# Windowed attention scored by half blocks of 320 keys, with start-up splits and tail loads in another order

## The chip, the cores and the metric

The kernel runs on one core of one Trainium2 chip. The metric is the device time of one execution in microseconds (us). Three executions of the kernel before took 2492.85, 2494.92 and 2496.40 us; the median, 2494.92 us, is the time that the forecast is made against.

## The reference, cut to what matters

One encoder layer is applied to two sequences (prompt and sample) of 2048 tokens by 1024 channels, all in float32.

- `h = rms_norm(x)`, then one projection of 1024 by 3328 gives q, k, v and a gate for two groups of heads.
- Group A (stage one of the kernel): 8 query heads and 2 key/value heads of 64 channels. A query sees the keys at most 128 tokens before or behind it. q and k are normalised and partly rotated; a learned sink per head joins the maximum and the denominator of the softmax.
- Group B (stage two): 8 heads, neighbourhood attention on a grid of 32 by 64 tokens with a learned bias.
- Each group's output is multiplied by SiLU of its gate; both together go through `w_out` and are added to x; then `x + (p @ w_ple) * sigmoid(x @ w_ple_gate)` (stage three).

The change is in group A:

```python
sc = einsum('bqkgd,bskd->bkgqs', qb, kb) * scale     # 128 queries, 384 keys
sc = where(abs(s - 128 - q) <= 128 and key exists, sc, -inf)
m = maximum(max(sc), sink);  e = exp(sc - m)
o = (e / (sum(e) + exp(sink - m))) @ vb
```

Of the 384 keys that a block of 128 queries is scored with, each query sees 257; 64 neighbouring queries see 320 between them.

## The kernel before, in words

Every float32 product is made of two or three products of a rounded part and a rest: an operand is split by ScalarE (ACT) into `hi`, and VectorE (DVE) or GpSimd (POOL) makes `lo = x - hi`. TensorE (PE) then multiplies hi by hi, hi by lo, and mostly lo by hi, into one PSUM tile.

**Stage one** (`f` from 0 to 31; 16 blocks of 128 tokens for each sequence, `s, t = divmod(f, 16)`). `proj_a(f)` is a generator that makes the projection of block f: 24 products of 256 columns for k and v (`pk`), 24 of 512 for q (`pq`), 24 of 512 for the gate (`pg`). It is the filler between the steps of attention, `unit_a(f, kv)`, one unit for each of the two key heads of a block. A unit has these steps: `sc(i)` (scores of one query head against 384 keys, two products, then on DVE mask and row maximum in `softmax`, L275), `exps` (L291 on ACT, denominator on DVE, gate factor g2 on POOL), `pt(j)` (four transposes of 128 by 128 for one block of keys, a copy on ACT and the rest on DVE into a `p_t` tile, L678 and L679), `po(j)` (two products of 512 columns with the values), `fin` (transposed gate, sums of two halves of rows on ACT and DVE, L698 to L702, store).

`PLAN_A` is an order written out by hand: a list of (share of the filler's cost, this or the previous unit, step, index). The main loop draws filler products until the share is reached and then emits the step, so that TensorE always has projection products between two steps. The order of TensorE's instructions is pinned to that emission. On the other engines the framework's scheduler may place an instruction earlier or later, unless `P` (keep in program order) or `behind` (not before the present product) fixes it. SyncE (SP) issues nearly all DMAs, in one queue.

PSUM has three groups of banks: `pj` (3 banks: projections), `sc` (3 banks, shared by `sc`, `pt` and `pgt`) and `ms` (2). With eight uses of `sc` in a unit, a score's bank is the one used three steps before: the third score's bank held the last `pt` of the unit before, the fourth's held the first score.

At an edge of a sequence (t = 0 or 15) two key blocks are there instead of three: 256 keys.

**Start.** SP loads x, the weights of `pk` (`wx`), of `pq` (`w_q`), the rows for the norms (`n`), the rotation tables (`cs`, `rw`), the weights of `pg` (`w_g`). `split_w` (L156 on ACT, L157 on DVE) splits each weight block. Block 0 and 1 make their `pk`, then their `pq`, then their `pg`.

**Stage two** (`f` from 32 to 95) works the same way with `proj_b` and `unit_b`; each unit loads its values (`vw`, L825) from DRAM. At the end of each stage two blocks are projected together (`paired`), so that the weights' tiles come free early.

**Tail.** While the last units of stage two run, `ple_ahead(n)` makes `p @ w_ple`, tile by tile of 512 tokens (8 groups `m` of 6 products), copies it from PSUM to an `ev` tile (L953) and stores it (`ple_d`, L954). Between these, `load_coming` loads the split blocks of `w_out` named a11, a12, a22 (L930), 512 KB each, one at every odd m.

Of the kernel before, what the change touches and what calls it, by code (L numbers as in the profile page):

```python
# [11 lines left out]
F32 = mybir.dt.float32  # L12
# [88 lines left out]
def emit(ctx, tc, io):  # L101
# [24 lines left out]
    nc.vector.tensor_tensor(out=wk[:, 0:1], in0=wkt[:, 0:1], in1=wkt[:, 1:2], op=ALU.mult)  # L126
    nc.vector.tensor_tensor(out=wk[:, 1:2], in0=wkt[:, 2:3], in1=wkt[:, 3:4], op=ALU.mult)
    nc.vector.tensor_scalar_mul(wk, wk, 0.125)
    nc.vector.memset(wk[0:16, 0:1], 0.125)
    nc.vector.memset(wk[64:80, 0:1], 0.125)  # L130
# [122 lines left out]
    def behind(ins):  # L253

        tc.add_manual_dep(ins.ins, last_pe[-1].name,
                          mybir.DependencyInfo(mybir.DependencyClass.NoSync, mybir.DependencyReason.DATA),
                          reason="behind the product")
# [14 lines left out]
    def softmax(i, ps, n, bias, sm):  # L272

        s = main.tile([128, 512], F32, tag="s", name="s", bufs=SB)
        nc.vector.tensor_tensor_reduce(out=s[:, :n], in0=ps[:, :n], in1=bias, scale=1.0, scalar=-3.0e38,  # L275
                                       op0=ALU.add, op1=ALU.max, accum_out=sm["mx"][:, i:i + 1])
        sm["s"].append(s)
# [4 lines left out]
    def exps(sm, n, fct, gs, sink=None):  # L282

        mx, nm, den, rd, ss = (sm[k] for k in ("mx", "nm", "den", "rd", "s"))
        if sink is None:
            nc.vector.tensor_scalar_mul(nm, mx, -1.0)  # L286
            yield
        else:
            nc.vector.scalar_tensor_tensor(out=nm, in0=mx, scalar=-1.0, in1=sink[1], op0=ALU.mult, op1=ALU.min)
        for n_, i in enumerate((0, 2, 1, 3) if sink is None else range(4)):  # L290
            ex = nc.scalar.activation(ss[i][:, :n], ss[i][:, :n], AF.Exp, bias=nm[:, i:i + 1],  # L291
                                      accum_out=den[:, i:i + 1])
            if sink is None and n_ == 0:
                P(ex)
        if sink is not None:
            es = ap.tile([128, 4], F32, tag="es", name="es", bufs=3)
            nc.vector.tensor_tensor(out=es, in0=sink[0], in1=nm, op=ALU.add)
            nc.scalar.activation(es, es, AF.Exp)
            yield
            nc.vector.tensor_tensor(out=den, in0=den, in1=es, op=ALU.add)  # L300
# [99 lines left out]
    raws_q += load_first(raw[:, 0:2], 2, 256, 512)  # L400
    for i in range(2):
        load_block(("n", 0, i), "s", SB)
    raws_q += load_first(raw[:, 2:4], 4, 256, 512)
# [14 lines left out]
    raws_q += load_first(main.tile([128, 2, 512], F32, tag="p_t", name="ws", bufs=3), 6, 256, 512)  # L418
    for j in range(KT // 2):
        split_w(w_q[j], raws_q[j], nw[:, j:j + 1])  # L420
    for i in range(2):
        square(0, i)
    for i in range(2):
        square(1, i)
# [15 lines left out]
    nc.sync.dma_start(snk[:, 0, :], io["sink"].partition_broadcast(128))  # L440
    nc.vector.tensor_scalar_mul(snk[:, 1, :], snk[:, 0, :], -1.0)
    tab = [ap.tile([128, 2, NT, 16], F32, tag="vp", name=f"tab{i}", bufs=3) for i in range(2)]
# [7 lines left out]
    mask = ap.tile([128, 384], F32, tag="vp", name="mask", bufs=3)  # L450
# [32 lines left out]
    def proj_a(f):  # L483
# [5 lines left out]
        for i, c in enumerate(project(pk, xr, lambda k, b: wx[:, k, b, :], 112)):  # L489
            if i in HS and early:  # L490
# [6 lines left out]
        nc.scalar.activation(sq2[:, :128], pk[:, 0:128], AF.Square)  # L497
        nc.vector.tensor_reduce(out=ssq[:, 8:10], in_=sq2[:, :128].rearrange("p (h d) -> p h d", d=HD),
                                op=ALU.add, axis=AX.X)
# [34 lines left out]
        for i, c in enumerate(project(pq, xr, lambda k, b: w_q[k][:, b, :], 215)):  # L534
# [6 lines left out]
            if i == PV:  # L541
                values()
# [98 lines left out]
    def prep_a(f):  # L641
        q = held[f][0]
        pqt = ptile([128, 512], "ms", "pqt")
        for i in range(4):
            tr(pqt[:, 128 * i:128 * i + 128], q[:, 2 * i:2 * i + 2, :].rearrange("p h d -> p (h d)"))
# [4 lines left out]
        return q1, q2  # L650

    def unit_a(f, kv):
        s, t = divmod(f, NT)
        _, gs, y = held[f]
        k0, k1 = max(0, t - 1), min(NT, t + 2)
        n = 128 * (k1 - k0)
        m0 = 128 * (k0 - t + 1)
        sm, prs, got = sm_tiles(), [], {}

        def sc(i):  # L660
            ps = ptile([128, 512], "sc", "sc")
            for j, q in enumerate(qs[f]):
                mm(ps[:, :n], q[kv][:, 128 * i:128 * i + 128], ks_a[:, kv, 128 * k0:128 * k1], j == 0, j == 1)
            softmax(i, ps, n, mask[:, m0:m0 + n], sm)
            if i == 3:
                got["ex"] = exps(sm, n, y[:, 11:12], gs[:, 256 * kv:256 * kv + 256],
# [3 lines left out]
        def pt(j):  # L670
            if j >= k1 - k0:
                return
            pt = ptile([128, 4, 128], "pt", "pt")
            for i in range(4):
                tr(pt[:, i, :], sm["s"][i][:, 128 * j:128 * j + 128])
            pr = main.tile([128, 2, 512], F32R, tag="p_t", name="pr", bufs=3)
            pf = pt.rearrange("p h q -> p (h q)")
            nc.scalar.copy(pr[:, 0], pf)  # L678
            nc.vector.tensor_tensor(out=pr[:, 1], in0=pf, in1=pr[:, 0].bitcast(F32), op=ALU.subtract)  # L679
            prs.append(pr)  # L680

        def po(j):
            if j == 0:
                got["po"] = ptile([128, 512], "ms", "po")
            if j < k1 - k0:
                v = vv[:, k0 + j, kv].rearrange("p a d -> p (a d)")
                for i in range(2):
                    mm(got["po"], v, prs[j][:, i], j == 0 and i == 0, k0 + j == k1 - 1 and i == 1)

        def fin(_):  # L690
# [4 lines left out]
            ph2 = got["po"].rearrange("p (i e q) -> p e i q", e=2, q=128)  # L695
            for e in range(2):
                a, z = 64 * e, 64 - 64 * e
                nc.scalar.copy(ot[a:a + 64], ph2[z:z + 64, e])  # L698
            for e in range(2):
                a = 64 * e  # L700
                nc.vector.tensor_tensor(out=ot[a:a + 64], in0=ph2[a:a + 64, e], in1=ot[a:a + 64], op=ALU.add)
# [106 lines left out]
    def unit_b(f):  # L808
# [25 lines left out]
        def sc(h):  # L834
# [5 lines left out]
            if h == 3:  # L840
                got["ex"] = exps(sm, n, hr_b[:, st:st + 1], gs)
# [92 lines left out]
    def ple_ahead(n, tail=False):  # L934

        load_p(n + 1)
        for m in range(KT):
            if m % 2:
# [12 lines left out]
            else:  # L951
                ev = ap.tile([128, TW], F32, tag=("ev", "sq")[m // 2 % 2], name="ev", bufs=2)
# [27 lines left out]
    for count, w, raws in ((24, (), ()), (24, w_q, raws_q), (10 ** 9, w_g, raws_g)):  # L980
        if w is w_q:
            for j in range(KT // 2, KT):
                split_w(w[j], raws[j], nw[:, j:j + 1])
# [12 lines left out]
    def paired(f, n):  # L996
# [7 lines left out]
        else:  # L1004
            load_early("p")
            load_coming(4)
# [9 lines left out]
        else:  # L1016
            for name in ("a11", "a12", "a22"):
# [256 lines left out]
def _band():  # L1274
    q = np.arange(128)[:, None]
    k = np.arange(384)[None, :]
# [71 lines left out]
```

## Time and profile before

| | |
|---|---|
| median of three runs | 2494.92 us |
| the profiled execution, whole time | 2497.78 us |
| its span in the profile | 2495.8 us |
| mean granted TensorE clock | 0.998 |
| stage one / two / tail and stage three | to about 765 / to about 1846 / to the end |
| DMA traffic | 438.86 MB, mean 176 GB/s |

The span is what the profile shows; 2.0 us of the execution's time lie around it. Busy shares of PE are modelled from pipelined products, so the rows to read are the distances between starts and the waits. In the chain of waits (the view that follows what ended last backwards), each row gives the start, the length and what it was spent on; a row with `x4` is four instructions in a row.

### The profile page before, as it was taken

Reading aid. Unit: us, or ns where it says so; the run is one execution under the profiler, and the core shown is the slowest. Engines: PE = TensorE matmul, PEld = TensorE weight load, DVE = VectorE, ACT = ScalarE, POOL = GpSimd, SP = SyncE. Lnnn points to the kernel's source line nnn. Section 1 sums busy time; section 2 is a strip of 40 time slices with the busy share of each in tenths; the row PEclk is TensorE's granted clock in tenths of the full one; section 3 lists DMA queues with packets and bytes.
Section 4 is the critical chain, followed back from the end, with each engine's and each line's share of the span. In section 5 each row is a group of like instructions: output and inputs, shape, how many; then the busy total and the mean of one; then the engine's idle time right before and its main releaser. Section 6 shows DMA issues by size and latency. Waiting matters only on the chain.

```text
span 2495.8 us, 39867 instructions
## 1 busy us (share of the span) xinstructions
PE 2474.3 (99%) x12920; PEld 2088.8 (84%) x12920; DVE 1732.5 (69%) x4274; ACT 1417.1 (57%) x3341; POOL 787.9 (32%) x1033
## 2 busy tenths in 40 slices
PE   9999999999999999999999999999999999999998
PEld 7888888888888888888888888888788888888887
DVE  6777777777775666666666676776546655687776
ACT  6677667767765566665566666665664222344443
POOL 4444444445444444444444443443110000000000
PEclk9999999999999999999999999999999999999999
DMA  5432233222254465556865666666978455756765
GB/s 199 138 118 94 87 92 102 90 92 91 88 183 140 146 197 178 166 182 187 276 184 182 184 206 197 199 203 215 307 240 278 156 171 176 265 171 219 244 225 168
DMA packets 246656, 438.86 MB, mean 176 GB/s; under 512 B 31920, under 2 KB 86320, under 8 KB 241200
## 3 DMA queue, kind: packets, MB, share of 16 engines
q1 hardware_dynamic: 246160, 436.30, 54.2%
q8 instruction: 103, 1.69, 0.3%
q14 instruction: 105, 0.86, 0.1%
q10 hardware_dynamic: 288, 0.01, 0.0%
HBM read 308.28 MB, written 133.19 MB: 177 GB/s over the span
## 4 chain that ended last, share of the span: by engine, by line
PE 93%; DMA 3%; DVE 2%; ACT 1%; issue 0%; POOL 0%; SPq 0%; DVEq 0%; ACTq 0%; POOLq 0%
PE pqk L260 14%; PE pvg L260 14%; PE acca L1171 13%; PE accc L1171 10%; PE pg L260 7%; PE pq L260 7%; PE scb L260 4%; PE ptb L263 3%; PE pob L260 3%; PE sc L260 3%; PE po L260 3%; PE pk L260 3%; PE pt L263 3%; PE pple L260 3%; DMA vw<-v_d 1%; DMA ple_d<-ev 1%
## 5 line engine op out<-in xcount | busy, mean ns | idle before, releaser
L291 ACT ACTIVATE s<-s,nm 128x384 f32<-128x384 f32 (+4 forms) x512 | 307.2, 601 | 323.9 <-DVE nm L286 195.1
L260 PE MATMUL pvg<-wb,xr 128*128 128x512 f32 x1536 | 461.5, 407 | 0.1
L260 PE MATMUL pqk<-wa,xr 128*128 128x512 f32 x1536 | 442.2, 410 | 0.0
L260 PEld LDWEIGHTS pqk<-wa,xr 128*128 128x128 f32 x1536 | 266.3, 189 | 36.9
L260 PEld LDWEIGHTS pvg<-wb,xr 128*128 128x128 f32 x1536 | 267.0, 189 | 31.8 <-DVE wb L157 0.8
L356 POOL TENSOR_TENSOR xr<-stx,xr 128x512 fp32r<-128x512 f32 x188 | 241.6, 1296 | 162.2 <-ACT xr L355 154.5
L1153 ACT CAST opd<-raw 128x512 fp32r<-128x512 f32 x224 | 131.5, 618 | 269.2 <-PE acca L1171 116.2
L1154 DVE TENSOR_TENSOR opd<-raw,opd 128x512 fp32r<-128x512 f32 x224 | 146.4, 685 | 144.2 <-ACT opd L1153 144.2
L260 PE MATMUL pg<-wb,xr 128*128 128x512 f32 x768 | 231.5, 409 | 1.0 <-DVE vv L506 1.0
L260 PE MATMUL pq<-wa,xr 128*128 128x512 f32 x768 | 222.1, 402 | 1.6 <-DVE wa L157 1.5
L275 DVE CUSTOM_DVE_ANT_0 s<-scb,bias 128x288 f32<-128x288 f32 (+3 forms) x256 | 141.9, 555 | 105.0 <-PE scb L260 102.5
L142 POOL TENSOR_TENSOR yb<-vrb,power 128x8 f32<-128x8 f32 x64 | 105.4, 1646 | 252.2 <-DVE vrb L747 239.5
L1171 PE MATMUL accc<-opd,wb 128*128 128x512 f32 x768 | 177.0, 389 | 0.2 <-DVE r L1215 0.2
L1171 PE MATMUL acca<-opd,wa 128*128 128x512 f32 x768 | 175.5, 389 | 0.0
L1171 PE MATMUL acca<-opd,s 128*128 128x512 f32 x768 | 175.4, 389 | 0.0
L1171 PEld LDWEIGHTS accc<-opd,wb 128*128 128x128 f32 x768 | 144.1, 188 | 30.5 <-DVE r L1215 0.6
L1171 PEld LDWEIGHTS acca<-opd,s 128*128 128x128 f32 x768 | 144.2, 188 | 29.9
L1171 PEld LDWEIGHTS acca<-opd,wa 128*128 128x128 f32 x768 | 144.1, 188 | 29.9
L873 DVE TENSOR_TENSOR otb<-pob,otb 64x512 f32<-64x512 f32 x128 | 88.1, 689 | 113.3 <-ACT otb L872 112.3
L260 PEld LDWEIGHTS pq<-wa,xr 128*128 128x128 f32 x768 | 140.3, 190 | 25.4 <-DVE wa L157 2.4
L260 PEld LDWEIGHTS pob<-p_t,vw 128*128 128x128 f32 (+2 forms) x832 | 132.4, 189 | 29.4 <-DVE p_t L854 5.1
L260 PEld LDWEIGHTS pg<-wb,xr 128*128 128x128 f32 x768 | 137.0, 189 | 21.9 <-DVE vv L506 1.5
(159 smaller groups left out, 5123.1 us busy)
## 6 DMA issues: line engine op xcount, KB each, us to landing
stx<-x_b SPq DMA_DIRECT2D x128, 256.0 KB
vw<-v_d SPq DMA_DIRECT2D x112, 256.0 KB
stx<-x_a SPq DMA_DIRECT2D x64, 256.0 KB
stn<-x_n SPq DMA_DIRECT2D x64, 256.0 KB
v_d<-vb SPq DMA_DIRECT2D x64, 256.0 KB
ple_d<-ev SPq DMA_DIRECT2D x64, 256.0 KB
xres<-x_r SPq DMA_DIRECT2D x64, 256.0 KB
x_d<-r SPq DMA_DIRECT2D x64, 256.0 KB
```

Of the source, the lines that this page charges most:

```text
L142: nc.gpsimd.tensor_tensor(out=y, in0=v, in1=power.broadcast_to([128, n]), op=ALU.pow)
L260: pinned(nc.tensor.matmul(out, lhsT, rhs, start=start, stop=stop))
L263: pinned(nc.tensor.transpose(out, in_, eye))
L275: nc.vector.tensor_tensor_reduce(out=s[:, :n], in0=ps[:, :n], in1=bias, scale=1.0, scalar=-3.0e38, op0=ALU.add, op1=ALU.max, accum_out=sm[ ...
L291: ex = nc.scalar.activation(ss[i][:, :n], ss[i][:, :n], AF.Exp, bias=nm[:, i:i + 1], accum_out=den[:, i:i + 1])
L356: low.tensor_tensor(out=lo, in0=raw, in1=hi.bitcast(F32), op=ALU.subtract)
L873: nc.vector.tensor_tensor(out=ot[a:a + 64], in0=pq[a:a + 64], in1=ot[a:a + 64], op=ALU.add)
L1153: P(nc.scalar.copy(hi, v))
L1154: P(nc.vector.tensor_tensor(out=lo, in0=v, in1=hi.bitcast(F32), op=ALU.subtract))
L1171: pinned(nc.tensor.matmul(ps, w[k][:, a, c:c + 128], o[:, b], start=i in (0, 1, 4) and k == 0 and j == 0, stop=k == 3 and j == 2, skip_gro ...
```

## The change

1. **Scores by half blocks.** A score step takes two heads by 64 queries (`pair`, `half`) instead of one head by 128 queries, and 320 keys instead of 384 (256 and 192 at the edges). `prep_a` writes the transposed queries in that order. Both halves of a pair lie in one tile of 640 columns (`s2`, tag `ev`, 3 buffers), second half behind the first. So columns 256 to 384 hold the last 64 keys of the first half and the first 64 of the second: one transpose serves both ("mixed"). A unit has 4, 4 and 2 transposes instead of 4, 4 and 4.
2. **Mixed block over all rows with zeros.** The third `p_t` tile takes rows 0 to 63 for the first half's columns and rows 64 to 127 for the second's; the rest was set to zero once. Its products run over all 128 rows. The values' products are two of 512 columns and eight of 256, instead of six of 512. Its copy and its rest are two instructions each, of 64 rows by 256 columns.
3. **Denominator.** The rows of a score are now (head, query) and those of the gate (half, query), so the sum with the sink is four small instructions on DVE instead of one; the sink's table is built with two copies. `fin` reads PSUM in runs of 64 columns instead of 128.
4. **Start.** The last two loads of `w_q` (512 KB each) go ahead of `n`, `cs`, `rw`; all eight `w_q` splits come before the squares; the five small instructions that make `wk` move from the beginning to behind these splits; the key sums of block 0 stand behind the split of `w_q[3]`.
5. **Values sooner.** In block 30 the values are taken five products earlier.
6. **Tail.** The four a11 loads are issued together with those of `w_ple`; the other eight follow at m = 3 and 7 of tiles 0 to 2 and m = 3 of tiles 3 and 4. The `ev` tiles have three buffers.

The core of the diff:

```diff
     def sc(i):
+        pair, half = divmod(i, 2)
+        a, z = span[half]
+        c0, n = 128 * t - 128 + 64 * half, z - a
...
-            mm(ps[:, :n], q[kv][:, 128 * i:128 * i + 128], ks_a[:, kv, 128 * k0:128 * k1], j == 0, j == 1)
-        softmax(i, ps, n, mask[:, m0:m0 + n], sm)
+            mm(ps[:, :n], q[kv][:, 128 * i:128 * i + 128], ks_a[:, kv, c0 + a:c0 + z], j == 0, j == 1)
+        softmax(i, ps, n, mask[:, a:z], sm, pairs[pair][:, 320 * half + a:320 * half + z])
...
     def pt(j):
-        for i in range(4):
-            tr(pt[:, i, :], sm["s"][i][:, 128 * j:128 * j + 128])
+        if j == 2:
+            for pair in range(2):
+                tr(pt[:r.stop, 128 * pair:128 * pair + 128], pairs[pair][:, 256:256 + r.stop])
+        else:
+            for x in range(c.start // 128, c.stop // 128):
+                half, pair = divmod(x, 2)
+                col = ((128, 384), (0, 512))[j][half]
+                tr(pt[:, 128 * x:128 * x + 128], pairs[pair][:, col:col + 128])
+        pr = p_rot[j]
...
     def po(j):
+        steps = ([(0, slice(0, 512))], [(-1, first)] * left + [(1, second)] * right,
+                 [(1, first)] * right + [(-1, second)] * left)[j]
+        for d, c in steps:
             for i in range(2):
-                mm(got["po"], v, prs[j][:, i], ...)
+                mm(got["po"][:, c], v, prs[j][:, i, c], ...)
...
     # exps, with a sink
-        nc.vector.tensor_tensor(out=den, in0=den, in1=es, op=ALU.add)
+        for half in range(2):
+            for e in range(2):
+                rows = slice(64 * e, 64 * e + 64)
+                nc.vector.tensor_tensor(out=rd[64 * half:64 * half + 64, e::2], in0=den[rows, half::2],
+                                        in1=es[rows, half::2], op=ALU.add)
...
     # start
+raws_q += load_first(raw[:, 2:4], 4, 256, 512)
+raws_q += load_first(main.tile([128, 2, 512], F32, tag="p_t", ...), 6, 256, 512)
 for i in range(2):
     load_block(("n", 0, i), "s", SB)
-raws_q += load_first(raw[:, 2:4], 4, 256, 512)
...
-raws_q += load_first(main.tile([128, 2, 512], F32, tag="p_t", ...), 6, 256, 512)
-for j in range(KT // 2):
-    split_w(w_q[j], raws_q[j], nw[:, j:j + 1])
+for j in range(KT):
+    split_w(w_q[j], raws_q[j], nw[:, j:j + 1], halves.append if j == 3 else lambda ins: ins)
...
     # proj_a
-        if i == PV:
+        if i == (PV if f not in last else PV - 5):
             values()
...
     # ple_ahead
-            if m % 2:
+            if m % 4 == 3 and (n < 3 or m == 3):
                 load_coming()
-                ev = ap.tile([128, TW], F32, tag=("ev", "sq")[m // 2 % 2], name="ev", bufs=2)
+                ev = ap.tile([128, TW], F32, tag=("ev", "sq")[m // 2 % 2], name="ev", bufs=3 - m // 2 % 2)
     # paired, at the end of stage two
             load_early("p")
-            load_coming(4)
+            load_early("a11")
+            load_coming(8)
```

More of the change, by code (lines that the diff above doesn't have):

```diff
@@ L981, in emit @@
         if w is w_q:
-            for j in range(KT // 2, KT):
-                split_w(w[j], raws[j], nw[:, j:j + 1])
             drain(first[0], 23)
@@ L1016, in paired @@
         else:
-            for name in ("a11", "a12", "a22"):
+            for name in ("a12", "a22"):
                 load_early(name)
```

115 lines of the change are left out of this document (69 added, 46 removed).

## The prediction, made before the change was run

> **What bounds the kernel now.** I read the page's busy times first, then the same by stretches of time.
>
> ```profile
> PE 2474.3 (99%) x12920; PEld 2088.8 (84%) x12920; DVE 1732.5 (69%) x4274; ACT 1417.1 (57%) x3341; POOL 787.9 (32%) x1033
> ```
>
> TensorE is busy for 99% of the span; VectorE comes next with 69%. An average over stages can hide a stage with another limit, so the stretch in the middle of stage one is read, and who made TensorE wait from 40 to 700 us.
>
> ```profile
> 100.00:200.00 100.00, 100.00 (x583) 87.80 (x582) 78.08 (x232) 71.24 (x189) 44.12 (x74) 1.00 0.36 120
> ```
>
> ```profile
> PE pt L263 <- DVE ot L702: 1.1, 1, 1.1
> PE pqt L263 <- DVE ks_a L480: 0.9, 1, 0.9
> PE sc L260 <- DVE pr L679: 0.3, 1, 0.3
> ```
>
> In stage one DVE is busy 78% and ACT 71%, TensorE all the time at full clock (1.00), and its waits come to 2.3 us in 660. So there **a product that is taken out is worth its full spacing**, as long as the others keep up. For the spacings I read the chain of waits, here one block of 128 tokens, from its `pq` at 201.24 to the next block's at 224.35: 23.1 us.
>
> ```profile
> 200.52 0.72 PE pk L260 x6
> 201.24 0.47 PE pq L260 x2
> ...
> 207.48 2.09 PE pq L260 x9
> ...
> 209.57 0.44 PE pt L263 x4
> ...
> 213.77 0.69 PE sc L260 x4
> ...
> 214.81 0.35 PE sc L260 x2
> ...
> 224.35 0.47 PE pq L260 x2
> ```
>
> A score product of 384 columns takes 0.174 us (0.69 by 4, 0.35 by 2), a transpose 0.11, a product of 512 columns 0.232 (2.09 by 9), one of 256 columns 0.12 (0.72 by 6). No row of stage one has 320 columns. Stage two has the neighbours; here the distance between two starts is the spacing.
>
> ```profile
> 1775.21 0.32 PE L260 MATMUL scb<-ks_b,q1b 128*128 128x360 f32 x1
> 1775.37 0.33 PE L260 MATMUL scb<-ks_b,q 128*128 128x360 f32 x1
> ...
> 1794.10 0.29 PE L260 MATMUL scb<-ks_b,q1b 128*128 128x288 f32 x1
> 1794.23 0.30 PE L260 MATMUL scb<-ks_b,q 128*128 128x288 f32 x1
> ```
>
> 0.16 us for 360 columns, 0.13 for 288. The cost goes by width, so 320 lies between; I take 0.146.
>
> **1 and 2, half blocks on TensorE.** There are 64 units (32 blocks by 2 key heads); 8 are at an edge, 56 inside. In a unit inside:
> - scores: 8 products by (0.174 - 0.146) = -0.224 us. Bounds: -0.11 with 360's price, -0.35 with 288's.
> - transposes: 10 instead of 12: -0.22.
> - values: four products of 512 columns become eight of 256. At 0.232 against twice 0.12 this adds 0.008 each; I take +0.02, bounds 0 and +0.05. The zeros are multiplied like anything else, so that they are zeros brings nothing.
>
> Together -0.424, by 56: **-23.7 us**. At an edge transposes and columns of the values stay as many; four products go from 256 to 192 columns, about 0.025 each by the slope above, so -0.1 by 8: -0.8. The queries' transposes stay as many and only write in runs of 64; I take 0.
>
> **3, what the other engines get.** The durations, from the groups by form between 100 and 650 us (the last row from the same view of 700 to 1900):
>
> ```profile
> L679 DVE TENSOR_TENSOR pr<-pt,pr 128x512 fp32r<-128x512 f32 x140 | 93.6, 682 | 16.7 <-ACT pr L678 16.4
> L275 DVE CUSTOM_DVE_ANT_0 s<-sc,mask 128x384 f32<-128x384 f32 x174 | 91.4, 553 | 6.4 <-PE sc L260 4.9
> L678 ACT CAST pr<-pt 128x512 fp32r<-128x512 f32 x140 | 82.1, 588 | 13.6 <-PE pt L263 7.0
> L701 DVE TENSOR_TENSOR ot<-po,ot 64x256 f32<-64x256 f32 x96 | 40.5, 422 | 1.4
> L698 ACT COPY ot<-po 64x256 f32<-64x256 f32 x96 | 34.5, 359 | 0.6
> L300 DVE TENSOR_TENSOR den<-den,es 128x4 f32<-128x4 f32 x48 | 8.2, 170 | 74.9 <-ACT es L298 74.9
> L275 DVE CUSTOM_DVE_ANT_0 s<-sc,mask 128x256 f32<-128x256 f32 x16 | 6.3, 421 | 0.9 <-PE sc L260 0.5
> ```
>
> ```profile
> L719 DVE TENSOR_TENSOR ks_b<-pktb,ks_b 64x256 fp32r<-64x256 f32 x128 | 79.8, 623 | 14.0 <-ACT ks_b L718 10.9
> ```
>
> DVE for each unit: four masked maxima shrink from 553 to about 487 ns (halfway between the two forms), -0.26; the mixed block's rest is two of 422 instead of one of 682, +0.16; the denominator's sum is four of 170 instead of one, +0.51. That is +0.41, or 0.8 us in a block that now lasts 22.3 us: DVE rises from 78 to about 85%. ACT: the mixed copy is two of 359 instead of one of 588, +0.13, while four exponentials over fewer columns give at least that back. Neither becomes the bound by its sum. But the scores share three PSUM banks with the transposes, and the third score of a unit takes the bank that the last rest (`pr`) of the unit before must have read:
>
> ```profile
> 212.59 0.68 DVE L679 TENSOR_TENSOR pr<-pt,pr 128x512 fp32r<-128x512 f32 x1
> 213.35 0.56 DVE L275 CUSTOM_DVE_ANT_0 s<-sc,mask 128x384 f32<-128x384 f32 x1
> ```
>
> DVE is done with that bank at 213.27; the third score starts at 214.12 (213.77 and two products). The **slack is 0.85 us**. After the change TensorE gets there 0.33 sooner (two transposes, four narrower products) and DVE some 0.2 to 0.4 later, so 0.1 to 0.3 are left. Behind a late `pr` on DVE stand the maxima of the scores, and the fourth score waits for the first of them. I take waits of 0.3 us in one unit of ten, **+2.0 us**; below zero it cannot go, since TensorE waits for almost nothing now.
>
> [...]
>
> **4, the start.** First TensorE's rows, then stretches of 2 us, then a row of the chain:
>
> ```profile
> 14.16 3.85 PE L260 MATMUL pq<-wa,xr 128*128 128x512 f32 x16
> 19.18 0.73 PE L260 MATMUL pq<-wa,xr 128*128 128x512 f32 x2 [1.16 <-DVE wa L157]
> ...
> 20.87 8.41 PE L260 MATMUL pq<-wa,xr 128*128 128x512 f32 x29 [0.29 <-DVE wa L157]
> 29.12 2.43 PE L260 MATMUL pg<-wb,xr 128*128 128x512 f32 x10
> ```
>
> ```profile
> 22.00:24.00 2.00, 2.00 (x6) 1.54 (x5) 0.29 (x1) 0.59 (x2) 1.66 (x6) 0.50 1.05 382
> ```
>
> ```profile
> 12.77 6.52 DMA ws<-w_in
> ```
>
> The 48 `pq` products take from 14.16 to 29.12, 14.96 us, where 48 by 0.232 is 11.14. Sixteen run, then TensorE stands because the last two blocks of `w_q`, issued at 12.77, land at 19.29; after that its clock is at 0.50 for a while, and 29 products take 8.41 instead of 6.73. Placed before `n`, `cs` and `rw` (1.3 MB, 3.4 us at the 382 GB/s of that row), these loads land at about 15, and DVE's splits, 0.7 us each like the L679 row of the same size, stay level with three products each and a start 2 us ahead of them. So **-3.8 us**; bounds -1.5 (half a gap stays, and with it the clock) and -4.3 (the `wk` instructions off DVE's first us). What is late next: the norms' rows land some 2.7 us later, and with them squares and values of block 0, which stand before the splits of `w_g`; the first of these must be done when `pg` starts, now at 25.3. I estimate the squares' end at 19, the values' at 20 and the first split's at 21.5, which leaves 4 us of cover. The five `wk` instructions, the key sums behind `w_q[3]`, the sink's copies and the new zeros go into idle time of DVE and POOL before 25 us; I take 0 for them, bound 1 us.
>
> [...]
>
> **5 and 6, the end of stage one and the tail.** From the waits of TensorE (700 to 1700, then 1700 to 1900), SP's rows and two stretches:
>
> ```profile
> PE pg L260 <- DVE vv L506: 1.0, 1, 1.0
> ```
>
> ```profile
> PE pob L260 <- DMA vw<-v_d: 3.7, 3, 2.8
> PE pple L260 <- ACT ev L953: 0.7, 1, 0.7
> ```
>
> ```profile
> 1736.00 2.33 SPq L930 DMA_DIRECT2D wa<-sp_oa  x4
> ...
> 1778.33 0.78 SPq L930 DMA_DIRECT2D wb<-sp_oa  x1
> 1779.20 1.98 SPq L825 DMA_DIRECT2D vw<-v_d  x3
> ```
>
> ```profile
> 1780.00:1790.00 10.00, 6.64 (x33) 4.87 (x33) 3.58 (x9) 5.48 (x15) 2.15 (x4) 0.94 1.03 337
> 1790.00:1800.00 10.00, 10.00 (x52) 8.53 (x51) 4.81 (x14) 6.00 (x15) 0.23 (x1) 0.88 0.61 198
> ```
>
> Five products sooner is 1.2 us, so the wait for `vv` of 1.0 goes: -1.0, bounds 0 and -1.0. In the tail the values of a unit of stage two are issued at 1779.20 right behind a load of w_out, with the DMA engines full (1.03), and land late: 3.7 us of waits, and a clock of 0.94 and 0.88 for 10 us each costs 0.6 and 1.2. With half as many such loads (0.5 MB each, 1.6 us at 337 GB/s) before that point, the values land 1.6 to 3.1 us sooner: I take the clock's 1.8 and 2.4 of the waits, less 1.2 for the two or three loads that move to later units, **-3.0**, bounds +1 and -5.5. The a11 loads already go out at 1736.00, ahead of all this; moved up they stand before at most one load of values on SP, 2.33 us of issuing: I take 0, bound +1. The third `ev` buffer: -0.5 of the 0.7.
>
> **The sum**: -23.7 - 0.8 + 2.0 - 3.8 - 1.0 - 3.0 - 0.5 = -30.8. The profiled execution took 2497.8 us (span 2495.8 and 2.0 around it): 2467.0. It lies 2.9 above the median of the runs; against that, 2494.9 - 30.8 = **2464 us**.
>
> **The rivals.**
> - *The banks eat it.* If DVE's lateness exceeds the slack in every unit by 0.3 us, 64 units lose 19 instead of 2: 2481. For it: only 0.1 to 0.3 of slack by the sum above. Against: a steady lateness would first use up the idle time that DVE has before each denominator (74.9 us before 48). Chance 0.12.
> - *Start and tail give nothing*: other loads come late in their place. -24.5 + 2.0 gives 2472. Chance 0.07.
> - [...] Chance 0.04.
> - *Slower.* Runs of 64 columns in `fin` and of 2 in the denominator cost as the scattered ks_b does (623 against 422 for the same size): +0.4 on DVE, about as much on ACT ahead of it, so the last `pr` is 1.1 later. Only 0.52 (0.85 - 0.33) can be had, so each unit waits 0.6, 38 us in all: -24.5 - 8.3 + 38, **2500**. It decides from 0.5 us of waiting per unit on. Against: ks_b's runs are far shorter. Chance 0.03.
> - *Not what it says*: narrower products that don't get cheaper. The 288 and 360 rows exclude it.
>
> The forecast itself keeps 0.74. Its own range is 2457 (scores at 288's price) to 2471 (tail +1, start at its bound); with the bank rival the range for 8 in 10 is 2456 to 2480. A difference of 0.2%, 5 us, is about what a measurement tells from none: faster 0.96, within 0.01, slower 0.03.
>
> **What would show it.** In the new profile: score products 0.146 apart; ten transposes in a unit; blocks 22.3 us apart in stage one; 48 `pq` products without a gap from 14 to 25 us and no stretch at 0.50; no wait for `vv` and under 1.5 us for `vw`. Waits of `sc` for DVE of 0.3 us in unit after unit would prove the bank rival; a block still 23 us long would make the prediction wrong.

## The result, and the profile after

The changed kernel takes **2493.0 us** (median of 12 runs, 2489.5 to 2495.6), the kernel before, run beside it, 2493.6 (12 runs, 2492.6 to 2496.5): a ratio of 0.9995 with a 95% interval of 0.9988 to 1.0002. Forecast was 2464. No difference can be told; some 30 us of expected gain are not there. The profiled execution took 2493.3 us (span 2491.5).

The first question is whether the products got cheaper at all. The page's busy line of the changed kernel, then the stretch 100 to 200 us by engines (columns as before):

```profile
PE 2463.9 (99%) x13048; PEld 2075.2 (83%) x13048; DVE 1751.8 (70%) x4532; ACT 1415.5 (57%) x3405; POOL 794.3 (32%) x1043
```

```profile
100.00:200.00 100.00, 99.38 (x609) 86.89 (x608) 81.62 (x271) 72.04 (x198) 47.16 (x77) 1.00 0.36 120
```

TensorE does 609 products in these 100 us instead of 583, but it is no longer busy without a break: 99.38 instead of 100.00. Who it waits for stands in the waits from 40 to 700 us, here as PE's weight loads (PEld) and then PE itself see them; the columns are the sum in us, how often, and the longest:

```profile
PEld sc L255 <- DVE mx L271: 14.0, 29, 0.9
```

```profile
PE pt L258 <- DVE ot L743: 2.9, 2, 1.5
PE sc L255 <- DVE mx L271: 1.3, 5, 0.6
```

A score product waits 29 times, about once in every inner block of stage one, for the running maximum (`mx`) of an earlier score. Which one, and why then, is read from the chain of waits of one block:

```profile
203.85 2.07 PE pq L255 x9
...
209.87 0.70 PE sc L255 x4
...
210.91 0.29 PE sc L255 x2
...
212.12 0.47 PE po L255 x4
...
218.15 0.45 PE pt L258 x4
218.64 0.04 issue
218.68 0.59 ACT pr L714
...
220.07 0.38 ACT pr L714
...
220.47 0.42 DVE pr L716
220.90 0.43 DVE pr L716
...
221.36 0.21 DVE ms_a L502
221.57 0.19 DVE ssq L507
221.76 0.06 DVE ee L504
...
221.85 0.49 DVE s L271
222.37 0.04 issue
222.41 0.57 PE sc L255 x2
...
226.70 2.08 PE pq L255 x9
```

Rows of PE alone show the forecast prices: two `sc` of 320 columns in 0.29 at 210.91 (0.145 each; over nine blocks the median distance of two such products is 0.148), four `po` of 256 columns in 0.47. The four `sc` at 209.87 take 0.70, which is 0.12 more: there the third score waits for the last rest, a small wait that comes back below. But from 218.6 to 222.4 the chain leaves PE. It goes through ACT's copies of the transposes, DVE's rests, three tiny statistics of the next block (`ms_a`, `ssq`, `ee`) and the masked maximum of the first score of the next block, and comes back at the **fourth** score, which uses that first score's bank. From one run of nine `pq` products to the next are 22.85 us (203.85 to 226.70); the mean over nine blocks is 22.83, where before it was 23.11 and the forecast said 22.3.

### The profile page after: what moved, and what is told of

Same layout as the page of the kernel before. It is cut to its first block, busy times and chain, and to the rows that moved or that the text cites. A ratio compares the mean times of both kernels' runs of the same rounds, so it can differ in the third digit from the quotient of the medians.

```text
span 2491.5 us, 40573 instructions
## 1 busy us (share of the span) xinstructions
PE 2463.9 (99%) x13048; PEld 2075.2 (83%) x13048; DVE 1751.8 (70%) x4532; ACT 1415.5 (57%) x3405; POOL 794.3 (32%) x1043
## 4 chain that ended last, share of the span: by engine, by line
PE 89%; DVE 5%; ACT 3%; DMA 2%; issue 1%; POOL 0%; SPq 0%; ACTq 0%; DVEq 0%; POOLq 0%
PE pqk L255 14%; PE acca L1211 14%; PE pvg L255 14%; PE accc L1211 10%; PE pg L255 6%; PE pq L255 5%; PE scb L255 4%; PE ptb L258 3%; PE pob L255 3%; PE po L255 3%; PE pple L255 3%; PE pt L258 2%; PE sc L255 2%; PE pk L255 2%; ACT pr L714 1%; DVE pr L716 1%
## 5 line engine op out<-in xcount | busy, mean ns | idle before, releaser
L287 ACT ACTIVATE s<-s,nm 128x320 f32<-128x320 f32 (+6 forms) x512 | 294.4, 576 | 316.1 <-DVE nm L282 195.7
L255 PEld LDWEIGHTS pq<-wa,xr 128*128 128x128 f32 x768 | 135.0, 189 | 17.5
L255 PEld LDWEIGHTS pg<-wb,xr 128*128 128x128 f32 x768 | 132.0, 189 | 18.4 <-DVE vv L518 1.9
```

The source lines that it names most:

```text
L255: pinned(nc.tensor.matmul(out, lhsT, rhs, start=start, stop=stop))
L287: ex = nc.scalar.activation(ss[i], ss[i], AF.Exp, bias=nm[:, i:i + 1], accum_out=den[:, i:i + 1])
```

## The experiments

Ratios are to the kernel before on the same chip, with 95% intervals. Times are medians.

**1 to 3: the parts alone.** The first has only the half blocks (parts 1 to 3 of the change), the second only the start (part 4), the third only parts 5 and 6 and the third `ev` buffer.

```diff
# first: the changed kernel without
-    raws_q += load_first(..., 6, 256, 512)      # ahead of n, cs, rw; all of part 4
-    if i == (PV if f not in last else PV - 5):  # part 5
-    if m % 4 == 3 and (n < 3 or m == 3):        # part 6
# second, third: the kernel before with these
```

> Parts 1 to 3 alone; start, values and tail as before. Theory A (the fourth score of a block's first unit waits about 0.45 us for its bank, so a block gains 0.28 instead of 0.82): blocks 22.83 us apart as after the change, and 5 to 9 us below before, less what single stalls take. Rival (the scores are worth the forecast 24 us and start or tail give it back): blocks 22.3 apart, 2471 or so.

> Part 4 alone. Theory A's reading of the start (the gap moves from pq to pg, since the splits of w_g begin behind the values of block 0): pg reached 4 us sooner, the third block's pk only about 2 sooner, and 1.5 to 2.5 us below before. Forecast as on record: 3.8 us below.

> Parts 5 and 6 alone. Theory (the loads of w_out go out on SP at the same moments as before, wherever they stand in the text, because the scheduler pulls them up): three of them right ahead of the values' load again, the wait for vw 2 us or more, and within 1.5 us of before. Forecast as on record: 4.5 us below.

Measured: 2494.5 us (1.0004, 0.9995 to 1.0012), 2495.5 (1.0003, 0.9994 to 1.0011) and 2494.7 (1.0001, 0.9993 to 1.0010). None of the three gives anything that can be told from zero; the blocks of the first are 22.83 apart like the changed kernel's. The first was expected 5 to 9 us lower and the second 1.5 to 2.5: both missed, the third came as expected. In the first one's profile stage one gains 3.1 us from f = 2 on; one stall at f = 25 takes 2.1 back (it comes up again below). So no part spoils another's gain: each lacks its own.

**4: the first value product ahead of the fourth score.** If only that one bank is missing, PE can do the product `po` first.

```diff
-    ... (0.14, 1, "sc", 3),
-    (0.14, 1, "rest", 1), (0.14, 0, "po", 0),
+    ... (0.14, 0, "po", 0),
+    (0.14, 1, "sc", 3), (0.14, 1, "rest", 1),
```

> The changed kernel with one step of PLAN_A moved: the first products with the values (po 0 of the unit before) stand before the fourth score instead of behind it, 0.46 us of work for TensorE while the bank comes free. Theory A: the wait of 0.28 to 0.5 us in each block goes, blocks 22.35 to 22.45 apart, 12 to 15 us below the changed kernel, about 2480. Rival (DVE has more work in stage one than it can do in 22.8 us a block, above all the four sums of the denominator): the wait turns up at another step and the blocks stay 22.8 apart.

Measured: 2492.5 us (0.9993, 0.9984 to 1.0002), blocks 22.97 apart, longer than without. A row of TensorE in this run, at the other boundary, that of the two units inside a block, shows what came instead:

```profile
210.89 0.54 PE L255 MATMUL sc<-ks_a,q 128*128 128x320 f32 x2 [0.39 <-DVE pr L716]
```

The wait at the block's boundary is gone, but half a block on the third score waits for a rest (0.39 us in this block, 10.3 us in 27 waits between 40 and 700 us). A likely reason, which no run isolates: the fourth score is later by that product, and so are its maximum, the exponentials and everything behind them on DVE. This simple fix fails; other places in PE's order were not tried. Two theories were left. B: DVE's in-order run over a whole unit sets the pace. C: only the stretch at the block's boundary does, from the second group of transposes to the first maximum.

**5 and 6: less work on DVE away from the boundary.** The denominators' four sums as one (5), or all of the denominators' arithmetic on GpSimd (6).

```diff
# 5
-            for half in range(2): for e in range(2): nc.vector.tensor_tensor(out=rd[...], in0=den[...], in1=es[...], ...)
+            nc.vector.tensor_tensor(out=rd, in0=den, in1=es, op=ALU.add)
# 6
-                    nc.vector.tensor_tensor(out=rd[...], in0=den[...], in1=es[...], op=ALU.add)
-        nc.vector.reciprocal(out=rd, in_=den)
-        nc.vector.tensor_scalar_mul(rd, rd, fct)
+                    nc.gpsimd.tensor_tensor(out=rd[...], in0=den[...], in1=es[...], op=ALU.add)
+            nc.gpsimd.tensor_tensor(out=rd, in0=rd, in1=inverse.broadcast_to([128, 4]), op=ALU.pow)
+            nc.gpsimd.tensor_scalar_mul(rd, rd, fct)
```

> The changed kernel with the four 64x2 sums of the denominators back as one 128x4 sum in the scores' own layout, which leaves out the reordering (each head's row is divided by another row's denominator). VectorE loses 3 x 0.17 = 0.5 us per unit; TensorE and ScalarE lose nothing. Blocks of the changed kernel are 22.83 us apart, their TensorE work without waits is 22.34 (22.83 less the 0.49 us wait of the fourth score product). Theory B (VectorE's in-order run from the denominators to the maxima, closed into a loop by the exponentials, sets the pace of a block): blocks 22.35 apart, 28 x 0.48 = 13 us less, 2480 us. Theory C (only the chain at the block's boundary counts: second group of transposes, ScalarE's copies, VectorE's rests, statistics, first maximum, fourth score): the sums lie ahead of VectorE's 0.43 us wait for ScalarE's copy and are swallowed by it: blocks 22.8 apart, 2491 to 2494 us.

> The changed kernel with the four sums, the reciprocal (as a power of -1) and the product with half the root moved from VectorE to GpSimd: the same numbers computed. VectorE loses 0.66 + 0.18 + 0.21 = 1.05 us per unit and its wait for the last exponential; GpSimd, 46% busy, gains some 2 us per unit, and the gate product behind it is due a whole unit later. Theory B: blocks 22.35 apart and no wait left at the fourth score, 2478 to 2481 us. Theory C: blocks 22.8, 2491 to 2494 us. If GpSimd's queue gets late (rotary of the keys and the second query copies stand behind it), products wait for kt or q and the blocks are 23 us or more apart.

Measured: 2488.7 us (0.9980, 0.9971 to 0.9989), blocks 22.75 apart, and 2487.5 (0.9975, 0.9965 to 0.9984), blocks 22.73. Twice as much work taken from DVE in 6 as in 5, and the same 0.1 us in a block; the wait for the maximum is still there (13.0 us in 27 waits, in both). Theory B falls. Theory C's times (2491 to 2494) are missed too, by 2 to 4 us: about half of what the two runs gain on the changed kernel (4.4 and 5.5 us) lies in the blocks (2.2 and 2.8), where the rest comes from stays open.

**7: one copy and one rest for the mixed block.**

```diff
-            parts = [(r, c, c)] if j < 2 else [(slice(64 * x, 64 * x + 64), c, ...) for x, there in ...]
+            parts = [(r, c, c)]
```

> The changed kernel with the mixed half block's copy and rest as one 128x256 instruction each instead of two of 64x256; this leaves out the second half block (its columns stay zero). ScalarE loses 0.38 and VectorE 0.43 us per unit, and both lie between the transposes and the first maximum. Both theories: the 0.49 us wait at the fourth score goes, blocks 22.35 apart, 2479 to 2481 us. If it stays at 22.8, the wait has nothing to do with the mixed copies.

Measured: 2473.4 us (0.9919, 0.9905 to 0.9933), blocks 22.45 apart. So the wait is bound up with what stands between the transposes and the first maximum. Of the 20 us against the changed kernel only some 11 are the blocks (0.38 by 28); some 3 each are two single stalls, at f = 15 and f = 25, that this run does without. It leaves out the second half block's values, so it is no version to use.

**8: the boundary reordered**, nothing taken away: each mixed half's rest right behind its own copy, and the three statistics emitted four products into `pq`, behind the first scores.

```diff
+        def square_sums():
-        P(nc.vector.tensor_scalar(out=ms, in0=ssq[:, 10:11], ...))
+            P(nc.vector.tensor_scalar(out=ms, in0=ssq[:, 10:11], ...))
...
+            if i == 4 and f > 1:
+                square_sums()
...
             for r, c, to in parts:
                 nc.scalar.copy(pr[r, 0, to], pt[r, c])
-            for r, c, to in parts:
                 nc.vector.tensor_tensor(out=pr[r, 1, to], ...)
```

> The changed kernel with nothing taken away, only reordered at the block's boundary: each mixed half's rest directly behind its own copy (the first rest 0.38 us sooner), and the three statistics instructions (0.5 us of VectorE) behind the next score products instead of ahead of the first maximum. Theory C: the chain is 0.5 to 0.9 us shorter, the wait of 0.49 goes, blocks 22.35 apart, 2480 us. Theory B: the same instructions stand in the loop, only in another order, so the wait turns up elsewhere: blocks 22.7 to 22.9 apart, 2490 to 2495 us.

Measured: 2483.5 us (0.9956, 0.9944 to 0.9969), blocks 22.46 apart: with the same instructions in another order most of the wait goes (22.37 is what is left without it, run 10). Theory C holds, theory B is out.

**9 and 10: the two halves of that reordering.** First only the rest behind its copy, then only the late statistics.

```diff
# 9
             for r, c, to in parts:
                 nc.scalar.copy(pr[r, 0, to], pt[r, c])
-            for r, c, to in parts:
                 nc.vector.tensor_tensor(out=pr[r, 1, to], ...)
# 10
+        def square_sums():
...
+            if i == 4 and f > 1:
+                square_sums()
```

> Only one half of the reordering: each mixed half's rest directly behind its own copy, the statistics left where they are. The second rest can end 0.4 us sooner (at 220.9 instead of 221.33 in the block quoted). Theory C (the boundary chain is short of 0.4 us in a block, the rest is TensorE's own 22.43): 22.45 to 22.55 apart, 2481 to 2484 us, about as much as both halves. If the statistics were the part that counts: 22.8, 2492 us.

> The other half alone: the three statistics instructions (0.5 us of VectorE) behind the next scores, copies and rests as in the changed kernel. Theory C: the first maximum comes 0.5 us sooner and the wait at the fourth score goes as well: 22.45 to 22.55 apart, 2481 to 2484 us. If the third bank, which the second rest frees, is what the score waits for, nothing: 22.8, 2492 us.

Measured: the rest behind its copy 2492.9 us (0.9995, 0.9986 to 1.0003), blocks 22.79; the late statistics **2480.2** (0.9947, 0.9934 to 0.9961), blocks 22.37. The first half missed its expectation. The rows of DVE in that run show why, and then TensorE's weight loads, 40 to 700 us:

```profile
221.26 0.49 DVE L271 CUSTOM_DVE_ANT_0 s<-sc,mask 128x320 f32<-128x320 f32 x1 [0.15 <-PE sc L255]
221.68 0.08 DVE L271 DVE_READ_ACCUMULATOR2_ANT mx<- 128x1 f32 x1
221.79 0.43 DVE L715 TENSOR_TENSOR pr<-pt,pr 64x256 fp32r<-64x256 f32 x1
```

```profile
PEld sc L255 <- DVE mx L271: 11.1, 29, 0.9
```

Once they were not tied together, the scheduler put other work between the two copies on ACT, and the first maximum ahead of the second rest on DVE (221.26 and 221.79). The wait for the first maximum is still there, only one score earlier: now the third score waits for it, and the fourth finds the bank that the rest has freed. The third score starts 0.06 us behind the readout of the first maximum at both boundaries, and inside the block (at 210.22) even before the second rest has ended (210.62). Per block it loses 0.10 us at this boundary and 0.35 at the one inside the block, about as much as before. In the run with the late statistics, DVE and then TensorE:

```profile
217.98 0.86 DVE L723 TENSOR_TENSOR pr<-pt,pr 64x256 fp32r<-64x256 f32 x2 [0.43 <-ACT pr L721]
218.87 0.49 DVE L271 CUSTOM_DVE_ANT_0 s<-sc,mask 128x320 f32<-128x320 f32 x1
219.28 0.08 DVE L271 DVE_READ_ACCUMULATOR2_ANT mx<- 128x1 f32 x1
```

```profile
219.41 0.39 PE L255 MATMUL pq<-wa,xr 128*128 128x512 f32 x1
219.64 0.45 PE L255 MATMUL sc<-ks_a,q 128*128 128x320 f32 x2
```

The first maximum follows the rests at once and is read out at 219.36; the fourth score starts at 219.64, 0.23 behind the product ahead of it, as if nothing had ever been in its way. Not all 13 us are the blocks': by the squares of `pq` on ACT, the eleven blocks from f = 4 to 15 gain 5.0 us, and f = 15 alone 3.4 more; outside f = 15 stage one gains some 10. At f = 15, in the changed kernel as in the one before, the store of `ms_a` stands on SP between two loads of rows for the norms (`stn`), and ACT waits 4.1 us (before 4.6) in its order for the second. With the late statistics that store comes behind both.

**11: the same move in the kernel before**, as a control.

```diff
# the kernel before, with square_sums as above
+            if i == 4 and f > 1:
+                square_sums()
```

> The kernel before with nothing but the late statistics. Theory C says that the wait at the fourth score was made by the change (its second copy and rest make the first maximum 0.44 us later, its shorter products call for it 0.37 us sooner, and before there was 0.5 us of room): TensorE of the kernel before waits for nothing there, so nothing comes of it, 2492 to 2496 us, blocks 23.1 apart. Rival: the statistics cost the kernel before as much, and the change only kept an old wait: 2481 to 2484.

Measured: 2495.3 us (1.0006, 0.9997 to 1.0014), blocks 23.11 apart, to the hundredth as before. In the steady blocks of the kernel before there was no wait to remove: **the change made it.** The sum alone would not have shown that, since two single stalls cancel in it: f = 15 takes 2.6 us less than before (the store named above), f = 25 takes 2.5 more.

**12: the edges.** Four edits away from the steady blocks.

```diff
-            drain(first[0], 23)
+            drain(first[0], 20)
             for j in range(KT):
                 split_w(w_g[j], raws_g[j], nw[:, j:j + 1], P)
+                if j == 3:
+                    drain(first[0], 3)
...
-        nc.vector.tensor_scalar_mul(hr_b[:, c], rs_b[:, c], 0.5)
+        nc.gpsimd.tensor_scalar_mul(hr_b[:, c], rs_b[:, c], 0.5)
...
-            if i == (PV if f not in last else PV - 5):
+            if i == (PV if f not in last and f != 2 * NT - 1 else PV - 5):
...
-            nc.sync.dma_start(w.bitcast(F32), parts_d[key])
+            behind(nc.sync.dma_start(w.bitcast(F32), parts_d[key]))
```

> The changed kernel with four edits outside the steady blocks, each readable at its own place of the trace: (1) the first four splits of the gate weights ahead of block 0's values in program order; (2) the half roots of the second stage on GpSimd behind the power they wait for, instead of on VectorE; (3) the early place of the values given to the last block of stage one (f = 31) as well, not only to f = 30; (4) the loads of the early tail blocks held behind the product at which they are written. Theory: the gap in the first gate products (0.77 us and what the clock loses behind it) goes, 1 to 2.5 us by the second block; the step of 2.1 us at f = 25 goes; the 1.5 us wait at the start of the last gate products goes; the 2.2 us wait for vw and the clock behind it go, 2 to 4 us. Together 6 to 9 us: 2484 to 2487 us. Rival: the waits turn up a few instructions later (keys for the start, the full DMA engines for the tail), and the time stays within 2 us of 2493.

Measured: 2484.9 us (0.9964, 0.9952 to 0.9977), blocks 22.82 apart as in the changed kernel. By the same landmarks against the changed kernel's profile: 1.9 us at the second block, of which 1.3 are given back by f = 2 (the fourth score of the first block waits 0.72 instead of 0.23); 2.8 at f = 25; 1.1 at the end of stage one; 3.3 in the tail, of which 1.4 are given back when stage three starts. All four places react, two of them in part.

**13 to 15: together.** The boundary of run 8 with the edges; the late statistics with the edges; and the latter with the denominators on GpSimd (in its expectation "the run before the last" is the second of these three).

```diff
# the changed kernel with the diffs of
+# 13: 8 and 12
+# 14: 10 and 12
+# 15: 10, 12 and 6
```

> The four edits of the run before and the reordered block boundary (rest behind its own copy, statistics behind the scores) together; the same numbers computed as in the changed kernel. If both theories hold they add, since they act at different places: 10 us from the boundary and 6 to 9 from the edges, 2474 to 2478 us. If the start or the tail give nothing, 2480 to 2484.

> The changed kernel with the late statistics (13 us by themselves) and the four edits at the edges (8 to 9 us by themselves), without the interleaved rests. The two act at different places, so they add: 2470 to 2473 us, blocks 22.37 apart. If the earlier blocks only reach the full DMA engines of the tail sooner, the tail gives part of it back: 2474 to 2477.

> The run before the last with the denominators on GpSimd as well. Where no product waits for VectorE any more, 1.05 us less of it per unit buys nothing: within 2 us of the run without (2470 to 2473). If there is still a hidden wait for VectorE in each block, 2 to 4 us less.

Measured: 2472.2 us (0.9917, 0.9903 to 0.9930), **2469.6** (0.9906, 0.9893 to 0.9920; blocks 22.36 to 22.38) and 2471.7 (0.9915, 0.9901 to 0.9928; blocks 22.36). The edges add to the boundary, and with both, 1.05 us less on DVE in each unit buys nothing: a hidden wait for DVE in the blocks doesn't show. The waits of TensorE in the best kernel, 40 to 700 us:

```profile
PE sc L255 <- DVE pr L723: 0.8, 2, 0.5
PE sc L255 <- DVE mx L271: 0.2, 1, 0.2
```

The best version has the changed kernel's products, copies and sums, every one of them, in another order; one small product moves from DVE to GpSimd.

## Why the prediction was wrong, point by point

By its profile the changed kernel is 4.3 us ahead (2495.8 - 2491.5), where 30.8 were forecast. Some 14 of the missing 26.5 us lie in the inner blocks: 28 times 0.28 us came, where 28 times 0.85 less 2.0 were forecast. The others are the start, the tail and single stalls.

**Parts 1 and 2, -23.7 and -0.8: the prices were right.** 0.148 us for 320 columns (forecast 0.146), ten transposes of 0.109, 0.118 for a value product of 256, with the mixed block's zeros (four in 0.47 us from 202.31 on) as without (four in 0.47 from 200.91 on). Once nothing waits, a block takes 22.37 (run 10), 0.74 less than before; forecast were 0.85, so 3 of the 23.7 us are not found even then. Nor is the -0.8 of the edges: f = 16 to 19, around the edge in the middle, take 88.0 us instead of 87.0.

**Part 3, +2.0 for DVE's lateness: this is the step that failed.** The waits cost 22.83 - 22.37 = 0.46 us in each inner block, where the forecast had 0.3 us in one unit of ten; the term should have been +10 (what run 10 gains in stage one outside f = 15) to +13 (0.46 over all 28 inner blocks). Of the 0.46, 0.39 are the fourth score at the boundary from one block to the next. The working measured the slack of one boundary (between the two units of a block) and one wait (third score for the last rest), 0.85 us. It names the other wait too, of the fourth score for the first maximum, but took no slack for it; and it did not look at the other boundary, where the three statistics stand ahead of that maximum. DVE before, then DVE after, both at that boundary:

```profile
201.23 0.69 DVE L679 TENSOR_TENSOR pr<-pt,pr 128x512 fp32r<-128x512 f32 x1 [0.45 <-ACT pr L678]
201.84 0.20 DVE L493 TENSOR_SCALAR ms_a<-ssq 128x1 f32<-128x1 f32 x1
201.96 0.28 DVE L498 TENSOR_REDUCE ssq<-sq 128x2 f32<-128x128 f32 x1
202.16 0.14 DVE L495 TENSOR_SCALAR ee<-ms_a 128x1 f32<-128x1 f32 x1
202.22 0.55 DVE L275 CUSTOM_DVE_ANT_0 s<-sc,mask 128x384 f32<-128x384 f32 x1
202.69 0.08 DVE L275 DVE_READ_ACCUMULATOR2_ANT mx<- 128x1 f32 x1
```

```profile
220.47 0.86 DVE L716 TENSOR_TENSOR pr<-pt,pr 64x256 fp32r<-64x256 f32 x2 [0.43 <-ACT pr L714]
221.36 0.21 DVE L502 TENSOR_SCALAR ms_a<-ssq 128x1 f32<-128x1 f32 x1
221.49 0.28 DVE L507 TENSOR_REDUCE ssq<-sq 128x2 f32<-128x128 f32 x1
221.68 0.15 DVE L504 TENSOR_SCALAR ee<-ms_a 128x1 f32<-128x1 f32 x1
221.85 0.49 DVE L271 CUSTOM_DVE_ANT_0 s<-sc,mask 128x320 f32<-128x320 f32 x1
222.27 0.08 DVE L271 DVE_READ_ACCUMULATOR2_ANT mx<- 128x1 f32 x1
```

And TensorE's first `pk` product of the same block and the fourth score, before and after:

```profile
196.92 1.34 PE L260 MATMUL pk<-wx,xr 128*128 128x256 f32 x10
...
203.30 0.51 PE L260 MATMUL sc<-ks_a,q 128*128 128x384 f32 x2
```

```profile
216.11 1.36 PE L255 MATMUL pk<-wx,xr 128*128 128x256 f32 x10
...
221.89 0.40 PE L255 MATMUL pq<-wa,xr 128*128 128x512 f32 x1
222.41 0.57 PE L255 MATMUL sc<-ks_a,q 128*128 128x320 f32 x2
```

Counted from that `pk`: before, the first maximum is read out at 5.85 (202.77) and the fourth score is due at 6.38, so there were 0.53 us of room. After, TensorE gets there at 6.01 (221.89 and one product of 0.23), 0.37 sooner, and the maximum is read out at 6.24 (222.35), 0.39 later: 0.76 where 0.53 was to be had. That is the same sum as in the prediction, with the numbers of the boundary that decides. It leaves 0.23; the loss is 0.39, since the score starts 0.06 behind the readout and its two products, after standing still, take 0.40 to the next product's start (222.41 to 222.81) where run 10 has 0.29. At the boundary that the prediction did measure, nothing is left of the slack either: of the 0.1 to 0.3 us that it expected to remain, none did, and the third score loses about 0.1 us there in each block (0.03 in run 10).

The 0.39 is more than the second rest's price. ACT is hardly later (the last rests start 4.36 behind `pk` instead of 4.31); two rests of 64 rows take 0.17 longer than one of 128 (0.86 against 0.69); and the stretch from the rests' end to the first maximum grows from 0.30 to 0.52 us. Before, `ms_a` starts 0.08 ahead of the rest's end and the maximum 0.08 ahead of the end of `ee`; after, both start 0.02 to 0.03 behind. That is 0.1 us at each of the two places, and all ten blocks between 100 and 330 us show the same (0.07 to 0.09 ahead before, 0.02 to 0.04 behind after); in run 7, where one rest of 128 rows stands there, `ms_a` starts 0.09 ahead of its end again (217.81 against 217.90). Why this overlap is lost, no run isolates.

*The rival that the banks eat it* (2481, chance 0.12) was nearest in kind. Together with the next one (start and tail give nothing) it would have given 2489, but no rival put the two together; that *Slower* (2500) lies nearer to the measured time than 2481 is chance, since the runs of 64 columns in `fin` cost DVE 0.42 us as before. The bank rival named the right resource, the third and fourth score's banks, and the wrong holder: it expected 0.3 us in every unit behind the rests; it was some 0.4 in every second unit behind the maximum. Its counter-argument, that DVE would first use up its idle time ahead of the denominators, is what the wait itself and runs 5 and 6 refute: that idle time lies elsewhere in the block, and more of it brought 0.1 us in a block.

**Part 4, -3.8: the gap closed and another opened.** The rows of TensorE, and the first two of ACT's that matter:

```profile
14.13 11.07 PE L255 MATMUL pq<-wa,xr 128*128 128x512 f32 x48
25.04 1.78 PE L255 MATMUL pg<-wb,xr 128*128 128x512 f32 x7
27.59 0.97 PE L255 MATMUL pg<-wb,xr 128*128 128x512 f32 x3 [0.77 <-DVE wb L152]
```

```profile
23.30 0.37 ACT L517 ACTIVATE vv<-pk,y 128x128 fp32r<-128x128 f32 x1 [1.69 <-DVE kt L541]
23.57 2.55 ACT L151 ACTIVATE wb<-ws,nw 128x512 fp32r<-128x512 f32 x4
```

All 48 products run without a gap, in the 11.1 us forecast. But the values of block 0 come at 23.3, not at 20, and the first split of `w_g` at 23.57, not at 21.5: the 4 us of cover that the prediction estimated were 1.5, and four splits didn't fit. Of the 3.8 some 1.8 are left in the profile at f = 2; run 2, by its times, can't tell it from zero.

**Part 5, -1.0: 0.** The wait for `vv` is still there, 1.5 us. The edit moves the values of block 30; those that the last `pg` waits for are of block 31, the second of the pair, which the condition `f in last` doesn't hold. The prediction took over from the change which block it was. With block 31 included (run 12) the wait is gone.

**Part 6, -3.0 and -0.5: nothing that run 3 can tell from zero.** SP's rows ahead of the late values in the changed kernel, then TensorE's wait:

```profile
1775.58 0.64 SPq L971 DMA_DIRECT2D wb<-sp_oa  x1
1776.31 1.66 SPq L866 DMA_DIRECT2D vw<-v_d  x3
```

```profile
PE pob L255 <- DMA vw<-v_d: 2.9, 3, 2.2
PE pple L255 <- ACT ev L994: 0.9, 2, 0.7
```

The loads of `w_out` are written at fewer places but are not pinned, and the scheduler draws them up to where their tiles are free: three still go out in the 4 us ahead of `vw`, as before. Held behind the product at which they are written (run 12), they spread, and the sum of that wait falls from 2.9 to 1.9. So of the 2.4 us of waits that were forecast 0.8 came (3.7 to 2.9), and of the clock's 1.8 nothing: from 1780 to 1790 us the granted clock is 0.83 and then 1.00, where it was 0.94 and 0.88; in run 12 it is 1.00 in both stretches. The third `ev` buffer leaves the wait for `ev` at 0.9, where before it was 0.7.

**Not foreseen at all**: at f = 25 DVE waits 3.8 us in its order for a power on GpSimd (2.0 before), and the transposes behind it, which costs 2.8 us; run 12 takes it away with one word. Why the wait is longer than before stays open.

What stays open: at the beginning of stage two the changed kernel's lead in its profile shrinks from 4.5 to 3.3 us; the 3 us of part 1; and the few us of runs 5 and 6 that aren't in the blocks.

## What to carry to other kernels

Where one engine is the bound at 100%, a product taken out is worth its price only up to the slack of the tightest loop through the other engines, so measure that slack at every boundary of the steady state (every bank, both units of a block), not at the first one found. When a shortened stage doesn't get shorter, look for the small in-order instructions that stand ahead of the one that frees a buffer; moving three of 0.2 us was worth 13, some 10 of it by this wait. And check in the profile that an edit touches the instance that waits, and that an unpinned transfer stays where the text puts it.

## What the runs showed of the hardware

Two DVE rests of 64 rows in place of one of 128 cost more at the boundary from block to block than the 0.17 us that their durations add (0.86 against 0.69): at the two places above, behind the rests and behind the statistics, the next instruction starts 0.02 to 0.04 us behind the end of the one ahead instead of 0.07 to 0.09 before it, 0.1 us of lost overlap each. And VectorE and ScalarE, busy for 82% and 72% of the stretch from 100 to 200 us in stage one, with VectorE idle for 30 us in ten blocks while the exponentials run (29.8 us in 21 waits between 100 and 330 us), still held up TensorE once in each block: the order of their instructions decided that, not their load (with the late statistics of run 10 the weight loads' wait for the maximum falls from 14.0 us in 29 to 1.7 in 2, while less work on VectorE in runs 5 and 6 leaves 13.0 in 27).

In the profiles of the kernel before and of the changed one, each loss of clock on the way is a stretch of 3.4 us at a granted clock of 0.50, so 1.7 us lost (before from 20.8 and from 1788.9 us on, after from 1785.9). In as long a stretch ahead of each, TensorE stood for 1.6, 2.7 and 2.2 us in all; what makes the clock fall, no run isolates.
